# 32 of 256 tokens of an expert layer by gathered rows, the other 224 densely with a fused activation pair

## The chip, the core and the metric

One core of a Trainium2 chip runs the whole program: two transformer blocks on 256 tokens of width 2048, in float32. The metric is the device time of one execution, the median of the runs. The profile is one further execution, taken by the hardware profiler.

## What is computed

The change sits in the last layer of the second block, an expert layer (PEER) with 16384 experts. Each expert is one row of `u_tab` and one row of `v_tab`, 2048 numbers each. Each token picks 16 experts for each of 8 heads, 128 in all:

```python
q = (x @ wq).reshape(B, S, PEER_HEADS, 2, half)
s = jnp.einsum('bshpd,pkd->bshpk', q, subkeys)
s1, i1 = lax.top_k(s[..., 0, :], PEER_TOPK)
s2, i2 = lax.top_k(s[..., 1, :], PEER_TOPK)
...                                   # 16 x 16 candidates, best 16: idx, top_s
gate = jax.nn.softmax(top_s, axis=-1)
ue = jnp.take(u_tab, it, axis=0)      # per token: its 128 rows
ve = jnp.take(v_tab, it, axis=0)
act = gelu(jnp.einsum('td,ted->te', xt, ue))
out = jnp.einsum('te,ted->td', gt * act, ve)
```

The layer's result is added to the residual stream, and a last norm follows.

## The kernel before, in words

Activations lie transposed: 128 features in the partitions, the 256 tokens along the free axis, 16 such tiles for the width of 2048. All large products go through `chunk` and `mm3`. `chunk` (L371 to L385) loads a weight block of 128 x 2048 in two halves on SyncE's queue (`raw`), and for each half makes an upper part `whi` (ScalarE's cast to fp32r, L380) and a rest `wlo` (VectorE's subtraction, L381). Activations are split the same way by `split` (L411 to L420) into an upper and a lower tile (`Ah`, `Al` or `Bh`, `Bl`). `mm3` then runs three fp32r matmuls of 256 columns for each of the 16 steps k: upper x upper (L391), upper weights x lower activations (L392), lower weights x upper activations (L393), all into one PSUM tile. So each step k loads the same upper weights twice and the lower ones once.

`raw`, `whi` and `wlo` have four buffers each (halves), which is two weight blocks. `chunk` is issued with a priority 2000 instructions ahead, so that loads, casts and subtractions run as early as a buffer is free. Otherwise an engine works in the order of the program.

Side work is queued as generators (`push`), and `tick(n)` (L326) issues about n units of it after a large product. A generator that yields `GAP` waits for the next large product.

The expert layer computes all 16384 experts for all tokens and multiplies by a gate matrix that is zero where a token did not pick an expert:
- `route` (L1446): 16 blocks of `w_q`, and for each head the best 16 of both halves on VectorE; `route_tail` (L1492) makes gates and expert numbers from them, as side work behind the first `w_u` blocks.
- `build_g` (L1572): the gate matrix, from one-hot matrices in f16, 16 tokens at a time (`NT`): four VectorE operations and 32 matmuls of 128 columns per tile, 16 tiles. It goes to DRAM as `gdr`. It is side work too, behind further `w_u` blocks.
- `peer_u` (L1604): one block of 128 experts: product, times the norm's factor (L1609, VectorE), gelu (L1611, ScalarE). What is made before the gate matrix is there is stored in DRAM (`stash`, 64 blocks) and loaded again later (`st`, L1656, POOL's queue).
- The main loop in `peer` (L1658 ff.): 8 groups of 16 blocks. Each block is multiplied by its gates `G` (L1651) and split into `A` tiles; groups 0 to 3 take all their blocks from the stash, groups 4 to 7 take theirs from `peer_u`. Then come 16 blocks of `w_v`, whose products are added to the residual `hT` (L1686, VectorE). There is one set of 16 `A` tiles, so that the splits of a group overwrite those of the last one.

Of the kernel before, what the change touches and what calls it, by code (L numbers as in the profile page):

```python
# [48 lines left out]
T8 = 2  # L49
PRE = (60, 64, 64, 64, 80, 96, 112, 128)  # L50
# [12 lines left out]
def _consts():  # L63
# [31 lines left out]
    put("bkt", oh, "A")  # L95
    return {"cst" + g: np.concatenate(c, 1) for g, c in cols.items()}
# [5 lines left out]
def pack(inp):  # L102
# [132 lines left out]
class Kern:  # L235
# [73 lines left out]
    # ---- small helpers  # L309
# [9 lines left out]
    def mmps(self):  # L319
        return self.psm.tile([128, 256], F32, name="mm")  # L320

    # ---- work that is issued between the large products
# [3 lines left out]
    def tick(self, n=1, gaps=True):  # L326
        """spend n on the queued work; what follows a gap waits for the next large product to be issued"""
# [59 lines left out]
    def mm3(self, p, w, x, first=True, last=True):  # L387
        nc = self.nc
        n = len(w)
        for k in range(n):  # L390
            nc.tensor.matmul(p, w[k][0], x[k][0], start=(first and k == 0), stop=False)  # L391
            nc.tensor.matmul(p, w[k][0], x[k][1], start=False, stop=False)  # L392
            nc.tensor.matmul(p, w[k][1], x[k][0], start=False, stop=(last and k == n - 1))  # L393
# [14 lines left out]
    def xtile(self, st, k):  # L408
        return (self.xp.tile([128, 256], F32R, name=f"{st}h{k}"), self.xp.tile([128, 256], F32R, name=f"{st}l{k}"))

    def split(self, st, k, src, gain=None):  # L411
        nc = self.nc
        h, l = self.xtile(st, k)
# [6 lines left out]
        return h, l  # L420
# [19 lines left out]
    def warm_sqrt(self):  # L440
        """the table of the square root is loaded here, ahead of the next rstd"""
# [18 lines left out]
    def log1pexp_neg(self, out, e):  # L460
        """out = log1p(e), 0 <= e <= 1"""
# [15 lines left out]
    def softplus_neg(self, out_log1p, x):  # L477
        """out_log1p = log1p(exp(-|x|))"""
# [6 lines left out]
    def columns(self, r):  # L485
        """the two token columns of a row vector that all partitions hold"""
# [8 lines left out]
    # ---- stage 1  # L495
# [54 lines left out]
    def compress(self, kcs):  # L550
        """hidden layers of the compressed keys in partitions 0..63, of the values in 64..127"""
# [4 lines left out]
        for l in range(16):  # L556
            w = []
            for nm, st in (("k", "h"), ("v", "l")):
                wt = self.xp.tile([128, 256], F32, name=f"B{st}{l}")
                nc.scalar.dma_start(wt, self.I["c1" + nm][l // 8][:, 256 * (l % 8):256 * (l % 8) + 256])  # L560
                w.append(wt)
            wts.append(w)
            if l % 4 == 3:
                yield
# [146 lines left out]
    def nsa_pipe(self):  # L711
        """scores run ahead of the probabilities, these ahead of the output of both heads of a query block"""
# [74 lines left out]
    def nsa_out(self, pair):  # L787
        """both heads of a block, in the two halves of the array's columns"""
# [21 lines left out]
    # ---- RG-LRU  # L810
# [61 lines left out]
    def norm_residual(self, acc, r, gpost, st, gnext, ssq):  # L872
        """h += acc * r * gpost; next operands = split(h * gnext)"""
# [90 lines left out]
    def ple_prep(self):  # L964
# [4 lines left out]
        for k in range(2):  # L969
            h = self.T([128, 256], f"ph{k}", dt=F32R, bufs=1)  # L970
            l = self.T([128, 256], f"pl{k}", dt=F32R, bufs=1)
            nc.scalar.copy(h, pT[:, k])
            nc.vector.tensor_tensor(l, pT[:, k], h, op=ALU.subtract)
            self.px.append((h, l))
# [27 lines left out]
    # ---- block 2 mixers  # L1002
# [6 lines left out]
    def sincos(self, ph, sn, cs, w):  # L1009
        """sin and cos of ph [128, w]; ph is reduced in place"""  # L1010
# [16 lines left out]
    def s5_setup(self):  # L1027
        """tables of the recurrence, its input and its output weights, kept in DRAM until the blocks need them"""
# [153 lines left out]
    def s5_output(self, b, half, X, Y, cw, gw, uT):  # L1182
        """issued amid the next half, when the products are long ready"""
# [124 lines left out]
    def mlstm_cell(self, h, q, k, v, so):  # L1308
# [3 lines left out]
        # state after chunk 0  # L1312
# [122 lines left out]
    # ---- PEER  # L1435
# [10 lines left out]
    def route(self):  # L1446
# [4 lines left out]
        self.gT = [B([128, 256], f"g{i}T", F16) for i in range(2)]  # L1451
        self.rv = [self.T([128, 2, 8, 16], f"rv{i}", bufs=1) for i in range(2)]
        self.ri = [self.T([128, 2, 8, 16], f"ri{i}", dt=U32, bufs=1) for i in range(2)]
        for h in range(8):
# [29 lines left out]
            self.later(rest)  # L1484

# [6 lines left out]
    def route_tail(self):  # L1492
# [52 lines left out]
        for tb in range(2):  # L1545
# [24 lines left out]
            yield  # L1570

    def build_g(self):  # L1572
# [10 lines left out]
        for tb in range(256 // NT):  # L1583
# [20 lines left out]
    def peer_u(self, i):  # L1604
        nc = self.nc
        p = self.mmps()
        self.mm3(p, self.chunk(self.I["w_u"][i]), self.xs)
        t = self.T([128, 256], "pu", pool=self.dp)
        nc.vector.tensor_tensor(t, p, self.rz, op=ALU.mult)  # L1609
        a = self.T([128, 256], "pa", bufs=3, pool=self.dp)  # L1610
        nc.scalar.activation(a, t, AF.Gelu)  # L1611
        return a

    def peer(self):
        nc = self.nc
        self.gdr = self.dr.tile([256 // NT, 128, 128, NT], F32, name="gdr")
        stash = self.dr.tile([PRE[2] // 4, 128, 4, 256], F32, name="stash")
        self.dp = self.pool("dp", 2)
        n = 0
# [114 lines left out]
```

## Time and profile before

| | |
|---|---|
| median of 3 runs | 3413.0 us (3411.52 to 3414.73) |
| span of the profiled execution | 3406.6 us (no other time of it is listed) |
| TensorE busy | 3358.2 us, 99% |
| VectorE busy | 2256.7 us, 66% |
| ScalarE busy | 1678.6 us, 49% |
| GpSimd (POOL) busy | 231.2 us, 7% |
| DMA | 647.75 MB, mean 190 GB/s |

A span runs from the first to the last instruction. PE is TensorE's matmul, PEld its weight load, which runs beside matmuls; DVE is VectorE, ACT ScalarE, POOL GpSimd, SP SyncE. The end of a matmul in the trace is modelled, and its row covers the way through the array, so the spacing of starts says more than the length. A plain f32 matmul is recorded as two. L with a number is a line of the kernel.

### The profile page before, as it was taken

To read this page: it belongs to the slowest core of one execution; us is meant where nothing else is said; L and a number is where in the kernel's file an instruction comes from. 1 tells how busy PE (TensorE), PEld (TensorE's weight loads), DVE (VectorE), ACT (ScalarE), POOL (GpSimd) and SP (SyncE) were. 2 spreads that over 40 slices of the span, in tenths; PEclk is the share of its full clock that TensorE was granted. 3 is DMA by queue.
4 is the path that set the end of the run, shared out by engine and by line. 5 is a ranking of instruction groups with operands and counts; after the bars stand their busy time and mean duration, and the time that the engine had idled before them with its cause. 6 is when DMAs were issued, how large, how long until landed. Compare 5 with 4: busy or idle time off the path is not lost.

```text
span 3406.6 us, 66485 instructions
## 1 busy us (share of the span) xinstructions
PE 3358.2 (99%) x27323; PEld 3267.6 (96%) x27323; DVE 2256.7 (66%) x3763; ACT 1678.6 (49%) x2419; POOL 231.2 (7%) x333
## 2 busy tenths in 40 slices
PE   8999989999999999999999999999999999999998
PEld 7888989999999999888999999999999999999998
DVE  5677786565756488989777976566555655555564
ACT  5567554454645454545554455544434444444343
POOL 2001120000000211000010000000000000000001
PEclk9999999999999999999999999999999999999999
DMA  8443646676766656554465666697676666666664
GB/s 270 126 126 119 181 143 206 203 220 185 229 183 203 184 163 191 159 160 151 138 181 171 209 218 224 229 343 234 189 232 181 185 207 184 208 183 184 182 185 137
DMA packets 197201, 647.75 MB, mean 190 GB/s; under 512 B 22736, under 2 KB 46816, under 8 KB 194848
## 3 DMA queue, kind: packets, MB, share of 16 engines
q1 hardware_dynamic: 171776, 574.69, 55.3%
q0 software_dynamic: 13552, 43.29, 3.7%
q10 hardware_dynamic: 11568, 25.52, 2.0%
q8 instruction: 214, 3.51, 0.4%
q14 instruction: 91, 0.75, 0.1%
HBM read 604.06 MB, written 38.30 MB: 189 GB/s over the span
## 4 chain that ended last, share of the span: by engine, by line
PE 57%; DVE 1%; issue 0%; ACT 0%; DVEq 0%; ACTq 0%
PE mm L391 18%; PE mm L392 18%; PE mm L393 17%; PE sm L1598 2%; PE oT L1192 1%; PE sm L1150 0%; PE sm L1475 0%; DVE hT L1693 0%; PE sm L1203 0%; PE sm L1373 0%; DVE s5Y L1170 0%; PE sm L1338 0%; PE sm L1325 0%; DVE wlo L381 0%; PE sm L1358 0%
## 5 line engine op out<-in xcount | busy, mean ns | idle before, releaser
L380 ACT CAST whi<-raw 128x1024 fp32r<-128x1024 f32 x1056 | 1103.9, 1046 | 1421.3 <-PE mm L392 1254.4
L381 DVE TENSOR_TENSOR wlo<-raw,whi 128x1024 fp32r<-128x1024 f32 x1056 | 1292.4, 1225 | 732.1 <-ACT whi L380 728.8
L391 PE MATMUL mm<-Bh,whi 128*128 128x256 f32 x4240 | 1207.6, 285 | 0.0
L392 PE MATMUL mm<-Bl,whi 128*128 128x256 f32 x4240 | 1201.2, 283 | 0.0
L393 PE MATMUL mm<-Bh,wlo 128*128 128x256 f32 x4240 | 1200.2, 283 | 0.0
L391 PE MATMUL mm<-Ah,whi 128*128 128x256 f32 x4176 | 1187.9, 286 | 12.5 <-ACT Ah L415 5.1
L392 PE MATMUL mm<-Al,whi 128*128 128x256 f32 x4176 | 1187.9, 285 | 2.2 <-DVE Al L419 2.0
L393 PE MATMUL mm<-Ah,wlo 128*128 128x256 f32 x4176 | 1185.2, 284 | 1.2 <-DVE wlo L381 1.2
L391 PEld LDWEIGHTS mm<-Ah,whi 128*128 128x128 f32 x4176 | 803.3, 193 | 23.1 <-issue 6.7
L391 PEld LDWEIGHTS mm<-Bh,whi 128*128 128x128 f32 x4240 | 813.9, 192 | 9.5 <-issue 9.3
L392 PEld LDWEIGHTS mm<-Bl,whi 128*128 128x128 f32 x4240 | 813.8, 192 | 2.3 <-issue 2.2
L393 PEld LDWEIGHTS mm<-Bh,wlo 128*128 128x128 f32 x4240 | 813.4, 192 | 1.1 <-issue 1.0
L392 PEld LDWEIGHTS mm<-Al,whi 128*128 128x128 f32 x4176 | 804.6, 193 | 7.1 <-DVE Al L419 2.8
L393 PEld LDWEIGHTS mm<-Ah,wlo 128*128 128x128 f32 x4176 | 804.6, 193 | 4.6 <-issue 2.0
L431 POOL TENSOR_TENSOR ssq<-ssq,sq 128x256 f32<-128x256 f32 x110 | 125.6, 1141 | 1477.4 <-ACT sq L429 1474.2
L1686 DVE TENSOR_TENSOR hT<-hT,mm 128x256 f32<-128x256 f32 x128 | 53.8, 420 | 88.2 <-PE mm L393 88.2
L1609 DVE TENSOR_TENSOR pu<-mm,rstd 128x256 f32<-128x256 f32 x128 | 54.1, 423 | 56.4 <-PE mm L393 56.4
L415 ACT CAST Ah<-pa 128x256 fp32r<-128x256 f32 x64 | 26.0, 406 | 83.9 <-DVE pa L1651 83.9
L1623 POOL DMA_DIRECT2D stash<-pa x64 | 34.7, 542 | 472.9 <-ACT pa L1611 353.0
L1598 PE MATMUL sm<-gB,gA 128*128 128x128 f16 x512 | 65.8, 297 | 0.0
L1611 ACT ACTIVATE pa<-pu 128x256 f32<-128x256 f32 x128 | 52.9, 413 | 24.3 <-DVE pu L1609 24.1
L1599 ACT ACTIVATE gt<-sm 128x512 f32<-128x512 f32 x64 | 63.2, 1090 | 2.1 <-PE sm L1598 0.9
(432 smaller groups left out, 2165.2 us busy)
## 6 DMA issues: line engine op xcount, KB each, us to landing
raw<-in_w_m SPq DMA_DIRECT2D x256, 512.0 KB, 4.4
raw<-in_w_u SPq DMA_DIRECT2D x256, 512.0 KB, 4.4
raw<-in_w_v SPq DMA_DIRECT2D x256, 512.0 KB, 4.3
raw<-in_w_z SPq DMA_DIRECT2D x156, 512.0 KB, 3.9
raw<-in_w_o SPq DMA_DIRECT2D x64, 512.0 KB, 3.7
raw<-in_w_pg SPq DMA_DIRECT2D x32, 512.0 KB, 4.5
raw<-in_w_q SPq DMA_DIRECT2D x32, 512.0 KB, 4.1
gdr<-gt ACTq DMA_DIRECT2D x16, 1024.0 KB, 4.3
```

What stands on the lines that cost most here:

```text
L380: nc.scalar.copy(hi, raw)
L381: nc.vector.tensor_tensor(lo, raw, hi, op=ALU.subtract)
L391: nc.tensor.matmul(p, w[k][0], x[k][0], start=(first and k == 0), stop=False)
L392: nc.tensor.matmul(p, w[k][0], x[k][1], start=False, stop=False)
L393: nc.tensor.matmul(p, w[k][1], x[k][0], start=False, stop=(last and k == n - 1))
L431: nc.gpsimd.tensor_tensor(st["acc"], st["acc"], st["last"], op=ALU.add)
L1598: nc.tensor.matmul(p[:, 128 * r:128 * r + 128], A[:, q, :, r], b[:, q, :, r], start=(i == 0), stop=(i == 1))
L1599: nc.scalar.activation(Gt[:, :, 4 * q:4 * q + 4].rearrange("p i t -> p t i"), p.rearrange("p (t i) -> p t i", t=4), AF.Copy, scale=1.0 / GSC)
L1609: nc.vector.tensor_tensor(t, p, self.rz, op=ALU.mult)
L1611: nc.scalar.activation(a, t, AF.Gelu)
L1623: nc.gpsimd.dma_start(stash[n // 4, :, n % 4], self.peer_u(n))
L1686: nc.vector.tensor_tensor(self.hT[:, nb], self.hT[:, nb], p, op=ALU.add)
```

## The change

224 tokens (`ND2`) go the dense way, the last 32 (`SP`) by gathered rows.

The dense way: the two parts of an activation now lie in one tile of 2 x 256. In the expert layer `mm2` takes the place of `mm3`: per step k one matmul of the upper weights over both parts (2 x 224 columns, into two areas of one PSUM bank) and one of the lower weights over the upper part (224 columns). The two areas are added afterwards: in `peer_u` by a ScalarE copy and a VectorE add, for `w_v` by two VectorE adds. The activations of the expert layer are normalized in advance and split anew after the last `w_q` block (`xu`). The gate matrix and the stash have 224 tokens; `st` has 3 buffers instead of 4 and is loaded on SyncE's queue.

The gathered way: the expert tables are passed a second time, as rows cut in four quarters of 512. A tile has 32 tokens x 4 quarters in its 128 partitions. For each of a token's 128 experts an indirect DMA on POOL gathers 128 quarter rows (256 KB), and VectorE makes a dot product of them (`u`) or adds them with a weight (`v`). That is 256 gathers, with six buffers, as side work behind the main loop's blocks (`tick(TSP)`). Between both halves come one product over the quarters, gelu and gates; at the end four transposes and four adds into `hT`.

The other stages keep `mm3`, with operands `x[:, 0]` and `x[:, 1]` of the new tile. The core of the diff:

```diff
+SP = 32
+ND2 = 256 - SP
+NQ = 128 // SP
+QW = 2048 // NQ
+NR = 6
+TSP = 1.6
...
+    out["u_rows"] = A(f["peer_u_2"][0]).reshape(16384 * NQ, QW)
+    out["v_rows"] = A(f["peer_v_2"][0]).reshape(16384 * NQ, QW)
...
+    def mm2(self, w, x, n):
+        nc = self.nc
+        p = self.psm.tile([128, 512], F32, name="mm")[:, :2 * n].rearrange("p (c t) -> p c t", c=2)
+        m = len(w)
+        for k in range(m):
+            nc.tensor.matmul(p, w[k][0], x[k][:, :, :n], start=(k == 0), stop=False)
+            nc.tensor.matmul(p[:, 0], w[k][1], x[k][:, 0, :n], start=False, stop=(k == m - 1))
+        return p
...
     def xtile(self, st, k):
-        return (self.xp.tile([128, 256], F32R, name=f"{st}h{k}"), self.xp.tile([128, 256], F32R, name=f"{st}l{k}"))
+        return self.xp.tile([128, 2, 256], F32R, name=f"{st}x{k}")
...
     def route(self):
...
+            for k in range(3 * h - 3, min(3 * h, KC)):
+                if k >= 0:
+                    xn.append(self.xp.tile([128, 2, 256], F32, name=f"Ax{k}")[:, 0])
+                    V.scalar_tensor_tensor(xn[k], self.hT[:, k], self.P("norm2_g_2", k), self.rz, op0=ALU.mult, op1=ALU.mult)
+        self.behind()
+        self.xu = [self.split("B", k, xn[k][:, :ND2]) for k in range(KC)]
+
+        def sparse_x():
+            p = self.ps()
+            for k in range(KC):
+                q, c = divmod(k, KC // NQ)
+                nc.tensor.matmul(p[SP * q:SP * q + SP, 128 * c:128 * c + 128], xn[k][:, ND2:], self.C("ident"), start=True, stop=True)
+            nc.scalar.copy(self.xsp, p[:, :QW])
+
+        self.later(sparse_x)
...
     def route_tail(self):
...
+        yield GAP
+        p = self.ps()
+        for i, src in enumerate((gt[:, 1].rearrange("p s h -> p (s h)"), *es)):
+            nc.tensor.matmul(p[:, 128 * i:128 * i + 128], self.C("rsel"), src, start=True, stop=True)
...
     def build_g(self):
...
-        for tb in range(256 // NT):
+        for tb in range(ND2 // NT):
...
     def peer_u(self, i):
         nc = self.nc
-        p = self.mmps()
-        self.mm3(p, self.chunk(self.I["w_u"][i]), self.xs)
-        t = self.T([128, 256], "pu", pool=self.dp)
-        nc.vector.tensor_tensor(t, p, self.rz, op=ALU.mult)
-        a = self.T([128, 256], "pa", bufs=3, pool=self.dp)
+        p = self.mm2(self.chunk(self.I["w_u"][i]), self.xu, ND2)
+        t = self.T([128, ND2], "pu", pool=self.dp)
+        nc.scalar.copy(t, p[:, 1])
+        nc.vector.tensor_tensor(t, t, p[:, 0], op=ALU.add)
+        a = self.T([128, ND2], "pa", bufs=3, pool=self.dp)
         nc.scalar.activation(a, t, AF.Gelu)
         return a
 
+    def sparse(self, gp):
...
+        def gather(n):
+            r = gp.tile([128, QW], F32, name="row", bufs=NR)
+            nc.gpsimd.indirect_dma_start(out=r, out_offset=None, in_=self.I["uv"[n // 128] + "_rows"],
+                                         in_offset=bass.IndirectOffsetOnAxis(ap=self.osp[:, n % 128:n % 128 + 1], axis=0))
+            rows.append(r)
+
+        n = 0
+        for s in range(256):
+            while n < min(256, s + NR):
+                gather(n)
+                n += 1
+            r = rows.popleft()
+            i = s % 128
+            if s < 128:
+                V.tensor_tensor_reduce(out=r, in0=r, in1=self.xsp, scale=1.0, scalar=0.0, op0=ALU.mult, op1=ALU.add,
+                                       accum_out=d[:, i:i + 1])
+            elif i:
+                V.scalar_tensor_tensor(acc, r, w[:, i:i + 1], acc, op0=ALU.mult, op1=ALU.add)
+            else:
+                V.tensor_scalar(acc, r, w[:, 0:1], None, op0=ALU.mult)
+            yield
+            if s == 127:
+                yield GAP
+                p = self.ps()[:, :128]
+                nc.tensor.matmul(p, self.C("same"), d, start=True, stop=True)
+                nc.scalar.activation(w, p, AF.Gelu)
+                V.tensor_tensor(w, w, self.gsp, op=ALU.mult)
+                yield
...
     def peer(self):
...
+        self.push(self.sparse(gp))
...
         def stashed(i):
-            st = gp.tile([128, 4, 256], F32, name="st", bufs=4)
-            nc.gpsimd.dma_start(st, stash[i])
+            st = gp.tile([128, 4, ND2], F32, name="st", bufs=3)
+            nc.sync.dma_start(st, stash[i])
             return st
...
                         gated(g, n % 16, self.peer_u(n))
                         n += 1
+                    self.tick(TSP)
...
             if g == 7:
+                self.flush()
                 self.warm_sqrt()
             for nb in range(16):
-                p = self.mmps()
-                self.mm3(p, self.chunk(self.I["w_v"][16 * g + nb]), hid)
+                p = self.mm2(self.chunk(self.I["w_v"][16 * g + nb]), hid, ND2)
...
-                nc.vector.tensor_tensor(self.hT[:, nb], self.hT[:, nb], p, op=ALU.add)
+                for c in range(2):
+                    nc.vector.tensor_tensor(self.hT[:, nb, :ND2], self.hT[:, nb, :ND2], p[:, c], op=ALU.add)
...
+                else:
+                    self.tick(TSP)
```

## Rows read from the trace of the kernel before

**Rows 1.** The page: span, and busy time of each engine.
```profile
span 3406.6 us, 66485 instructions
...
PE 3358.2 (99%) x27323; PEld 3267.6 (96%) x27323; DVE 2256.7 (66%) x3763; ACT 1678.6 (49%) x2419; POOL 231.2 (7%) x333
```

**Rows 2.** The page: the chain that ended last, by line.
```profile
PE mm L391 18%; PE mm L392 18%; PE mm L393 17%; PE sm L1598 2%; PE oT L1192 1%; PE sm L1150 0%; PE sm L1475 0%; DVE hT L1693 0%; PE sm L1203 0%; PE sm L1373 0%; DVE s5Y L1170 0%; PE sm L1338 0%; PE sm L1325 0%; DVE wlo L381 0%; PE sm L1358 
```

**Rows 3.** Stretches: us, busy PE PEld DVE ACT POOL (counts), granted clock, DMA share, GB/s.
```profile
1864.00:1910.00 46.00, 46.00 (x386) 46.00 (x385) 45.93 (x197) 24.33 (x29) 3.78 (x7) 1.00 0.59 180
1910.00:1970.00 60.00, 60.00 (x504) 60.00 (x503) 55.74 (x72) 26.55 (x38) 5.96 (x11) 1.00 0.73 222
...
2210.00:3390.00 1180.00, 1180.00 (x9832) 1179.63 (x9831) 672.83 (x868) 496.29 (x630) 35.06 (x44) 1.00 0.66 204
...
2214.00:2299.00 85.00, 85.00 (x710) 85.00 (x710) 56.87 (x93) 38.42 (x55) 7.05 (x13) 1.00 0.98 344
```

**Rows 4.** Timeline of TensorE in the main loop: start us, length us, line.
```profile
2999.93 0.28 PE L391 MATMUL mm<-Ah,whi 128*128 128x256 f32 x1
...
3011.93 0.28 PE L392 MATMUL mm<-Al,whi 128*128 128x256 f32 x1
```

**Rows 5.** Timeline: weight loads of plain f32 matmuls of 512 columns.
```profile
44.22 0.19 PEld L529 LDWEIGHTS sm<-t,cstA 128*128 128x128 f32 x1 [0.24 <-issue]
44.65 0.19 PEld L529 LDWEIGHTS sm<-t,cstA 128*128 128x128 f32 x1 [0.24 <-issue]
```

**Rows 6.** Timeline and lengths (ns, min/median/max) of matmuls of 128 columns.
```profile
1971.77 1.00 PE L1598 MATMUL sm<-gB,gA 128*128 128x128 f16 x7
...
L1598 PE MATMUL sm<-gB,gA x512: 285/297/304, 1970.5 to 2204.1; 128*128 128x128 f16 x171
...
1772.90 0.83 PE L1475 MATMUL sm<-parD,rq 128*128 128x128 f32 x6
...
L1475 PE MATMUL sm<-parD,rq x64: 272/275/348, 1772.6 to 1860.3; 128*128 128x128 f32 x64
```

**Rows 7.** Timeline of VectorE: a turn of groups, an add, a reduce's end.
```profile
2464.22 1.23 DVE L381 TENSOR_TENSOR wlo<-raw,whi 128x1024 fp32r<-128x1024 f32 x1 [0.54 <-ACT whi L380]
2465.36 2.43 DVE L416 TENSOR_TENSOR Al<-st,Ah 128x256 fp32r<-128x256 f32 x7
...
2474.47 0.75 DVE L1651 TENSOR_TENSOR st<-st,G 128x256 f32<-128x256 f32 x2
...
1869.91 0.60 DVE L1500 TENSOR_TENSOR rcd<-rv,rv 128x448 f32<-128x448 f32 x1
...
130.06 0.08 DVE L752 DVE_READ_ACCUMULATOR2_ANT mn<- 128x1 f32 x1
```

**Rows 8.** Groups at 2210 to 3390 us: count, busy us, mean ns, idle before.
```profile
L381 DVE TENSOR_TENSOR wlo<-raw,whi 128x1024 fp32r<-128x1024 f32 x407 | 498.4, 1225 | 342.0 <-ACT whi L380 342.0
L380 ACT CAST whi<-raw 128x1024 fp32r<-128x1024 f32 x407 | 426.1, 1047 | 578.4 <-PE mm L392 537.2 <-issue 21.6 <-DMA raw<-in_w_v 14.4
...
L1656 POOL DMA_DIRECT2D st<-stash x16 | 8.5, 535 | 205.4 <-DVE Al L416 193.3 <-DMA gdr<-gt 7.7 <-issue 4.5
```

**Rows 9.** Waits: TensorE's of the span, POOL's in the main loop.
```profile
PE mm L391 <- ACT Ah L418: 4.6, 1, 4.6
...
POOL st L1656 <- DVE Al L416: 193.3, 10, 88.1
```

**Rows 10.** DMA at 2400 to 2600 us, then 2214 to 2300: us to landing.
```profile
DMA packets 12720, 40.69 MB, mean 203 GB/s; under 512 B 1296, under 2 KB 3344, under 8 KB 12702
...
raw<-in_w_v SPq DMA_DIRECT2D x69, 512.0 KB, 4.2
...
DMA packets 14354, 29.32 MB, mean 341 GB/s; under 512 B 1266, under 2 KB 9202, under 8 KB 14345
...
raw<-in_w_v SPq DMA_DIRECT2D x20, 512.0 KB, 6.7
...
st<-stash POOLq DMA_DIRECT2D x4, 512.0 KB, 6.6
```

More of the change, by code (lines that the diff above doesn't have):

```diff
@@ L95, in _consts @@
     put("bkt", oh, "A")
+    t, q = p % SP, p // SP
+    put("rsel", (np.arange(128)[:, None] == 128 - SP + t[None, :]).astype(np.float32), "P")
+    put("same", (t[:, None] == t[None, :]).astype(np.float32), "P")
+    put("qcol", q.astype(np.float32)[:, None], "P")
     return {"cst" + g: np.concatenate(c, 1) for g, c in cols.items()}
@@ L319, in mmps @@
     def mmps(self):
-        return self.psm.tile([128, 256], F32, name="mm")
+        return self.psm.tile([128, 512], F32, name="mm")[:, :256]
     def push(self, gen, q=0):
@@ L390, in mm3 @@
         for k in range(n):
-            nc.tensor.matmul(p, w[k][0], x[k][0], start=(first and k == 0), stop=False)
-            nc.tensor.matmul(p, w[k][0], x[k][1], start=False, stop=False)
-            nc.tensor.matmul(p, w[k][1], x[k][0], start=False, stop=(last and k == n - 1))
+            nc.tensor.matmul(p, w[k][0], x[k][:, 0], start=(first and k == 0), stop=False)
+            nc.tensor.matmul(p, w[k][0], x[k][:, 1], start=False, stop=False)
+            nc.tensor.matmul(p, w[k][1], x[k][:, 0], start=False, stop=(last and k == n - 1))
+    def mm2(self, w, x, n):
[6 more added lines that the diff above has]
+        return p
     def blocks(self, srcs, x, first=2):
@@ L556, in compress @@
         for l in range(16):
[L557 to L562, printed above, removed]
+            wt = self.xp.tile([128, 2, 256], F32, name=f"Bx{l}")
+            for s, nm in enumerate("kv"):
+                nc.scalar.dma_start(wt[:, s], self.I["c1" + nm][l // 8][:, 256 * (l % 8):256 * (l % 8) + 256])
+            wts.append(wt)
             if l % 4 == 3:
@@ L576, in compress @@
             for s in range(2):
-                nc.tensor.matmul(p[64 * s:64 * s + 64], blk[:, l, s], wts[l][s], start=(l == 0), stop=(l == 15))
+                nc.tensor.matmul(p[64 * s:64 * s + 64], blk[:, l, s], wts[l][:, s], start=(l == 0), stop=(l == 15))
         hid = self.T([128, 256], "chid", bufs=1)
@@ L969, in ple_prep @@
         for k in range(2):
[L970 to L974, printed above, removed]
+            x = self.T([128, 2, 256], f"px{k}", dt=F32R, bufs=1)
+            nc.scalar.copy(x[:, 0], pT[:, k])
+            nc.vector.tensor_tensor(x[:, 1], pT[:, k], x[:, 0], op=ALU.subtract)
+            self.px.append(x)
     def ple_proj(self, half):
@@ L1611, in peer_u @@
         nc.scalar.activation(a, t, AF.Gelu)
         return a
+    def sparse(self, gp):
+        nc = self.nc
+        V = nc.vector
+        d = self.T([128, 128], "spd", bufs=1, pool=gp)
+        w = self.T([128, 128], "spw", bufs=1, pool=gp)
+        acc = self.T([128, QW], "spa", bufs=1, pool=gp)
+        rows = deque()
+        def gather(n):
[24 more added lines that the diff above has]
+                V.tensor_tensor(w, w, self.gsp, op=ALU.mult)
+                yield
+        yield GAP
+        p = self.ps()
+        nb = QW // 128
+        for i in range(nb):
+            nc.tensor.transpose(p[:, 128 * i:128 * i + 128], acc[:, 128 * i:128 * i + 128], self.C("ident"))
+        for i in range(nb):
+            h = self.hT[:, i:KC:nb, ND2:]
+            V.tensor_tensor(h, h, p[:, 128 * i:128 * i + 128].rearrange("p (q t) -> p q t", q=NQ), op=ALU.add)
+        yield
@@ L1614, in peer @@
     def peer(self):
         nc = self.nc
[L1616 to L1617 removed]
+        NB = ND2 // NT
+        self.gdr = self.dr.tile([NB, 128, 128, NT], F32, name="gdr")
+        stash = self.dr.tile([PRE[2] // 4, 128, 4, ND2], F32, name="stash")
         self.dp = self.pool("dp", 2)
+        self.ctab = dict(self.ctab)
+        self.load_tabs(self.dp, "P")
+        self.gsp = self.T([128, 128], "gsp", bufs=1, pool=self.dp)
@@ L1639, in peer @@
         gp = self.pool("gp", 2)
-        GP = 256 // NT // 8
+        self.push(self.sparse(gp))
         def load_g(g, i, eng):
             if i == 0:
-                Gs[g] = gp.tile([128, 256 // NT, 16, NT], F32, name="G")
-            b = slice(GP * i, GP * i + GP)
-            eng.dma_start(Gs[g][:, b], self.gdr[b, :, 16 * g:16 * g + 16].rearrange("b p i t -> p b i t"))
+                Gs[g] = gp.tile([128, NB, 16, NT], F32, name="G")
+            b = slice(2 * i, min(2 * i + 2, NB))
+            if b.start < NB:
+                eng.dma_start(Gs[g][:, b], self.gdr[b, :, 16 * g:16 * g + 16].rearrange("b p i t -> p b i t"))
         def gated(g, j, a):
```

13 lines of the change are left out of this document (11 added, 2 removed).

## The prediction, made before the changed kernel ran

> **What bounds the kernel now.** I read the page first, then the chain, then a table of stretches, then single matmuls. The page has TensorE busy for 99% of a span of 3406.6 us [rows 1]; since a busy matmul row also covers waiting inside the array, that alone is no proof. The chain of waits gives the three matmul lines of `mm3` 53% of the span, and everything else in it is small [rows 2]. By stretches, TensorE is busy without a gap in the expert layer (its main loop is 2210 to 3390 us), at a granted clock of 1.00, the upper level of 2.4 GHz, while VectorE is busy 57% of its main loop and the DMA engines 66% [rows 3]. The timeline shows why: one matmul starts every 0.12 us without exception (2999.93 to 3011.93 us: 100 starts, 120.0 ns) [rows 4]. A weight block has 48 of them, 5.76 us. 256 blocks (1474.6 us) and the 512 one-hot products of `build_g` (at 117 ns, 60 us) make 1535 us; that is the layer. So time is worth what it saves TensorE here, as long as nothing else becomes late.
>
> What sets the 120 ns? Plain f32 matmuls of 512 columns start every 430 ns, two passes of 0.42 ns a column, and the load of the next 128 weight columns is hidden [rows 5]. A single-pass matmul of 256 columns would so need 108 ns. Matmuls of 128 f16 columns (54 ns of streaming) still start 117 ns apart ((1.00 - 0.297)/6), and plain ones of 128 columns (107 ns) 111 ns apart ((0.83 - 0.275)/5) [rows 6]. So each 128-column weight load holds its matmul to 111 to 120 ns, and shorter ones gain nothing below that.
>
> **The products.** Per step k, 3 loads with 768 columns become 2 loads with 448 and 224. The wide one: 448 x 0.42 = 188 ns, above the load, which it hides (200 if the 12 ns by which 120 exceeds 108 are a fixed charge per matmul). The narrow one: 94 ns of streaming, below the load of the next weights: 120 ns, the row of its own kind (112 to 120). So 308 ns instead of 360 (bounds 300 to 320), and 52 x 16 x 256 blocks = **-213 us** (-246 to -164). A block takes 4.93 us.
>
> By the Trainium skill, page "TensorE: Matmul & The Clock Gate", section "Back-to-back issue gap", a warm gap is N/2.4 + 2.5 ns: 109 ns before, 285 ns per step after. The trace has 120 where it says 109, so the load it leaves out does count. Its result is the third rival.
>
> **The dense rest.** `build_g` makes 14 tiles, not 16: 64 products less, -7.5 us. New on TensorE: 16 f32 products for `sparse_x`, 3 for the routing, 4 transposes and one more, about 48 passes at 0.112 = +5.4. TensorE's floor: 3406.6 - 213 - 7.5 + 5.4 = 3191.5 us.
>
> **What must stay hidden.** VectorE's recorded durations overlap: a `wlo` of 1.23 us lets the next start after 1.14, seven splits of 256 columns take 2.43 us (0.335 each), an add of 448 columns is 0.60 long, 0.52 by that overlap, and a reduce reads its accumulator in 0.08 more [rows 7]. So: split, gate or add of 224 columns 0.30 to 0.33; a gathered row's dot product 0.69 (0.61 + 0.08); its weighted add 0.61 to 0.67. `tick(1.6)` puts 1.6 of these, 1.1 us, behind each block, about 162 blocks for the 258 steps. VectorE per ticked block: `w_v` 2.28 + 2 x 0.33 + 1.1 = 4.04 us; `w_u` 2.28 + 3 x 0.30 + 1.1 = 4.28; `w_v` of the groups that also gate stashed blocks 4.64. Against 4.93 that is 82 to 94%: hidden on average, but the cover is thin, where before a `w_v` block left half of VectorE free.
>
> Five things come through:
> - The operands `xu` overwrite those of the last `w_q` block, so the first `w_u` block waits for its splits. The same kind of hand-over cost 4.6 us once [rows 9]: **+4.6** (0 to 15).
> - Route tail: VectorE is full at 1864 to 1910 (45.9 of 46) and nearly so to 1970 [rows 3]. Its 18.5 blocks could save 15 us; VectorE lets through 4. **+11** (0 to 15).
> - Four groups of stashed blocks: 16 splits follow each other at the turn of a group; they took 9.1 us (2465.36 to 2474.47) [rows 7] and the next group's last step came just in time. With 9.9 us for two blocks, less the lead, and sparse steps between: 2 us each, **+8** (0 to 25). In this the moved loads count: `st` goes from POOL, where it waited 193 us in all [rows 9] with nothing behind it, to SP with one buffer fewer; behind it queue the `raw` loads, which ACT's cast, `wlo` and L393's successor wait for. Only the fourth load of a group can wait, for the first quad's splits.
> - The weight ring. Four `raw` halves serve two blocks: landing, cast (1.05), `wlo` (1.2) must fit in 9.86 us instead of 11.5. Traffic rises: 256 gathers of 262 KB, 1.6 per block, are 85 GB/s on top of 213 for weights and some 14 for G (14.7 MB over the loop): 310. Landing was 4.2 us at 203 GB/s and 6.7 at 341 [rows 10], so about 6.2 here: 6.2 + 1.05 + 1.2 [rows 8] = 8.5, which leaves 1.4 for queueing behind a 0.7 us sparse step. At 344 GB/s TensorE had no gap [rows 3], but with 11.5 us. I take 0.15 us per ticked block, **+24** (0 to 110).
> - Sparse steps wait for gathers, and `wlo` queues behind them. No indirect load is in the trace. Below: a POOL issue, 0.54 us [rows 8]; above: issue and landing one after the other, 0.54 + 6.6 = 7.1 [rows 8, 10]. Six rows are in flight, so I take 1.2 us each against a need of one per 3.2 us: hidden, **+2** for the first ones.
>
> The page "DMA: Bandwidth & Descriptors" of the Trainium skill, section on the SWDGE path, has 2.0 us + bytes/436e3 per such DMA, an estimate of 2.6 us here; no run yet shows one, and by it too the gathers would keep up.
>
> Elsewhere `x[:, 0]` and the wider PSUM tile change addresses only; ACT, busy 496 of 1180 us [rows 3], gets one short copy per `w_u` block and stays below 60% of the shorter loop.
>
> Sum: 3191.5 + 4.6 + 11 + 8 + 24 + 2 = 3241 us of span. The median of the runs, 3413.0, is 6.4 above the profiled span (no time of that execution itself is listed): **3248 us**.
>
> **Rivals.**
> 1. *The narrow matmul loses its single pass* (slower). All single-pass rows have 256 columns; none is narrower, so no row excludes it. For: nothing but that gap. Against: f16 and plain f32 keep their cost per column at 128. Done as plain f32 it would be two records of 188 ns, +256 ns on 4096 steps: 4297 us; one record of 188: 3526. It decides from 160 ns per narrow matmul (165 us / 4096 = 40 above 120).
> 2. *The ring or VectorE binds.* Landing of 7 us and 2 us of queueing make 11.2 per two blocks, 5.6 per block: 162 x (0.67 - 0.15) = +84: 3332 us. For: the cover computed above. Against: no gap at 344 GB/s.
> 3. *Loads don't bind.* 672 x 0.42 = 282 ns per step: 106 us less, 3141 us. Against: the floor of [rows 6]. The gap rule of the Trainium skill quoted above ("TensorE: Matmul & The Clock Gate") would come out beside it, at 285 ns.
> 4. *The gathers don't keep up* (slower in the end). If issue and landing follow each other, 256 x 7.1 = 1818 us instead of 823: 4243 us. It decides from 3.86 us per gather ((823 + 165)/256). Against: six buffers.
>
> **Numbers.** Forecast 0.62, ring 0.18, loads free 0.06, narrow pass 0.07, gathers 0.07 (half of it beyond 3.86 us). Forecast's own range 3190 to 3300; with rivals 2 and 3: 3140 to 3350. Under 0.2% (7 us) can't be told from no change. Faster 0.62 + 0.18 + 0.06 + 0.02 = 0.88, same 0.02, slower 0.10.
>
> **What would show it.** Wide matmuls 188 ns ahead of the next start, narrow ones 112 to 120; TensorE's gaps in the main loop under 5%, at group turns and behind `wlo`; VectorE near 85% there; gathers at one per 3.2 us, landing under 10 us; `raw` landing near 6.2. A narrow matmul over 160 ns, or sparse steps waiting on DMA for most of the loop, would make the forecast wrong.

## The result, and the profile after

The changed kernel took 3510.4 us (3508.9 to 3513.9), the kernel before 3412.3 us on the same chip: a ratio of 1.029, interval 1.028 to 1.031. It is slower by 98 us; forecast were 165 less.

First the page of the changed kernel: span, busy times, three of the rows by fortieths, and the two groups of matmuls with the most idle time before them.

```profile
span 3508.3 us, 59745 instructions
...
PE 3261.7 (93%) x23207; PEld 3084.0 (88%) x23207; DVE 2456.9 (70%) x4306; ACT 1700.8 (48%) x2558; POOL 514.2 (15%) x573
...
PE   8999989999999999999998999558999757999998
...
POOL 2001210000000120000100001672000573000002
PEclk9999999999999999999999999769999878999999
...
L415 PE MATMUL mm<-Bx,wlo 128*128 128x224 f32 x2048 | 574.3, 280 | 147.7 <-DVE wlo L393 116.0
...
L415 PE MATMUL mm<-Ax,wlo 128*128 128x224 f32 x2048 | 548.3, 268 | 28.2 <-DVE wlo L393 18.0
```

TensorE's work fell by 97 us, but it is busy only 93% of the span, against 99% [rows 1]. The loss is not spread: the row PE has two holes, and in the same two places POOL is busy and the granted clock drops. The narrow matmul, which alone needs the low half `wlo`, had 176 us of idle time before it (147.7 + 28.2), most of them waiting for `wlo`. Away from the holes, a timeline of TensorE (start us, length us) answers [rows 4]:

```profile
3099.90 0.38 PE L414 MATMUL mm<-Ax,whi 128*128 128x448 f32 x1
3100.11 0.26 PE L415 MATMUL mm<-Ax,wlo 128*128 128x224 f32 x1
3100.22 0.37 PE L414 MATMUL mm<-Ax,whi 128*128 128x448 f32 x1
3100.43 0.26 PE L415 MATMUL mm<-Ax,wlo 128*128 128x224 f32 x1
3100.53 0.38 PE L414 MATMUL mm<-Ax,whi 128*128 128x448 f32 x1
```

Two steps take 0.63 us here (3099.90 to 3100.53), with 0.21 from the start of a wide matmul to the next and 0.10 to 0.11 from a narrow one. Over the 639 steps at 3000 to 3200 us the mean is 313 ns, against 360. The dense part does what the change says. Now three stretches of equal length (the columns are those of [rows 3]); the first two are the holes:

```profile
2200.00:2390.00 190.00, 106.25 (x401) 91.38 (x402) 126.23 (x325) 38.02 (x66) 139.33 (x134) 0.70 0.87 284
2750.00:2940.00 190.00, 110.14 (x490) 97.66 (x490) 136.57 (x199) 44.22 (x74) 146.91 (x122) 0.76 0.82 257
3000.00:3190.00 190.00, 190.00 (x1215) 181.21 (x1214) 127.05 (x171) 96.69 (x133) 0.00 (x0) 1.00 0.69 219
```

190 us hold 1215 matmuls where nothing is late; the holes have 401 and 490. At the full rate these would have taken 63 and 77 us, so 127 + 113 = 240 us are lost there. TensorE stands idle for 164 of them (84 + 80); the other 76 are longer matmuls, at a granted clock of 0.70 and 0.76. VectorE is busy for only 66% and 72% of the holes, and yet it is what TensorE waits for. Its timeline shows how that goes together (in brackets the idle time before an instruction, and what ended it):

```profile
2329.26 1.22 DVE L393 TENSOR_TENSOR wlo<-raw,whi 128x1024 fp32r<-128x1024 f32 x1
2330.40 0.68 DVE L1685 CUSTOM_DVE_ANT_0 row<-row,xsp 128x512 f32<-128x512 f32 x1
...
2331.44 0.69 DVE L1685 CUSTOM_DVE_ANT_0 row<-row,xsp 128x512 f32<-128x512 f32 x1 [0.35 <-DMA row<-in_u_rows,osp]
...
2332.82 0.69 DVE L1685 CUSTOM_DVE_ANT_0 row<-row,xsp 128x512 f32<-128x512 f32 x1 [0.68 <-DMA row<-in_u_rows,osp]
...
2336.14 0.69 DVE L1685 CUSTOM_DVE_ANT_0 row<-row,xsp 128x512 f32<-128x512 f32 x1 [2.63 <-DMA row<-in_u_rows,osp]
...
2336.81 0.69 DVE L1685 CUSTOM_DVE_ANT_0 row<-row,xsp 128x512 f32<-128x512 f32 x1
...
2337.48 0.69 DVE L1685 CUSTOM_DVE_ANT_0 row<-row,xsp 128x512 f32<-128x512 f32 x1
...
2338.10 1.22 DVE L393 TENSOR_TENSOR wlo<-raw,whi 128x1024 fp32r<-128x1024 f32 x1
```

Six dot products stand between two low halves, three of them wait for their gathers, and the second `wlo` runs 8.84 us after the first, where TensorE needs one every 2.5 us. The second `wlo` could have run long before: ScalarE had made the upper parts of both halves by 2325.29 us.

```profile
2323.32 1.97 ACT L392 CAST whi<-raw 128x1024 fp32r<-128x1024 f32 x2
```

The written program puts 1.6 sparse steps behind each block of two low halves. But VectorE's queue isn't in the written order, against what the section on the kernel before says of the engines: the language's scheduler lays it out, and here the sparse steps stand ahead of their places. All 128 dots run at 2190 to 2390 us and the weighted adds at 2750 to 2940 us, with mostly 3 to 6 of them between two low halves. Groups and waits of the first hole, and one gather at its shortest:

```profile
L1685 DVE CUSTOM_DVE_ANT_0 row<-row,xsp 128x512 f32<-128x512 f32 x121 | 80.9, 692 | 66.0 <-DMA row<-in_u_rows,osp 56.8 <-issue 8.3 <-DVE spd L1685 0.7
...
L1673 POOL DMA_INDIRECT row<-in_u_rows,osp x117 | 127.7, 1091 | 37.7 <-issue 29.9 <-DVE spd L1685 6.5 <-DVE st L1751 0.6
...
PE mm L415 <- DVE wlo L393: 47.1, 15, 7.7
...
2241.93 0.95 POOL L1673 DMA_INDIRECT row<-in_u_rows,osp  x1 [0.30 <-issue]
```

121 dots have 81 us of work and 66 us of waiting; POOL spends 1.09 us on a gather and 0.32 idle before it, 1.25 in all at best. With the stores of stashed blocks in the same queue one gather comes every 1.56 us (190/122: these 117 and the first 5 of `v`), and VectorE could use one every 0.67. POOL is at its own pace here: of the 38 us idle before gathers, 30 have no cause that the profile shows, and only 6.5 are waits for a dot that frees a row.

By the Trainium skill, page "PSUM — Partial Sum Buffer", section "Engine vs sequencer instructions", VectorE's queue is strictly first in, first out. The trace agrees: for 2.63 us VectorE stood before a dot whose gather had not landed, while the `wlo` behind it had its data since 2325.29.

### The profile page after: what moved, and what is told of

It is laid out like the page before. It is cut to its first block, busy times and chain, and to the rows that moved or that the text cites. A ratio compares the mean times of both kernels' runs of the same rounds, so it can differ in the third digit from the quotient of the medians.

```text
span 3508.3 us, 59745 instructions
## 1 busy us (share of the span) xinstructions
PE 3261.7 (93%) x23207; PEld 3084.0 (88%) x23207; DVE 2456.9 (70%) x4306; ACT 1700.8 (48%) x2558; POOL 514.2 (15%) x573
## 4 chain that ended last, share of the span: by engine, by line
PE 43%; DVE 5%; DMA 4%; issue 4%; POOL 3%; ACT 0%; DVEq 0%; POOLq 0%; SPq 0%; ACTq 0%
PE mm L414 21%; PE mm L415 10%; PE mm L403 3%; PE mm L404 3%; PE mm L405 3%; POOL row L1673 3%; DMA row<-in_v_rows,osp 2%; DVE wlo L393 1%; PE sm L1646 1%; PE oT L1214 1%; DMA row<-in_u_rows,osp 1%; DVE spa L1688 1%; DMA st<-stash 0%; DVE Ax L441 0%; DVE row L1685 0%
## 5 line engine op out<-in xcount | busy, mean ns | idle before, releaser
L415 PE MATMUL mm<-Bx,wlo 128*128 128x224 f32 x2048 | 574.3, 280 | 147.7 <-DVE wlo L393 116.0
L414 PE MATMUL mm<-Bx,whi 128*128 128x448 f32 x2048 | 707.3, 400 | 1.6 <-ACT whi L392 0.9
L414 PE MATMUL mm<-Ax,whi 128*128 128x448 f32 x2048 | 661.3, 382 | 16.5 <-DVE spa L1688 10.8
L403 PE MATMUL mm<-Bx,whi 128*128 128x256 f32 x2192 | 625.1, 285 | 0.0
L404 PE MATMUL mm<-Bx,whi 128*128 128x256 f32 x2192 | 621.6, 284 | 0.0
L405 PE MATMUL mm<-Bx,wlo 128*128 128x256 f32 x2192 | 620.9, 283 | 0.0
L403 PE MATMUL mm<-Ax,whi 128*128 128x256 f32 x2128 | 608.4, 288 | 13.2 <-ACT Ax L440 5.1
L404 PE MATMUL mm<-Ax,whi 128*128 128x256 f32 x2128 | 608.3, 286 | 3.1 <-DVE Ax L444 3.0
L405 PE MATMUL mm<-Ax,wlo 128*128 128x256 f32 x2128 | 605.7, 285 | 1.2 <-DVE wlo L393 1.2
L415 PE MATMUL mm<-Ax,wlo 128*128 128x224 f32 x2048 | 548.3, 268 | 28.2 <-DVE wlo L393 18.0
L415 PEld LDWEIGHTS mm<-Bx,wlo 128*128 128x128 f32 x2048 | 422.0, 206 | 163.8 <-DVE wlo L393 128.6
L414 PEld LDWEIGHTS mm<-Bx,whi 128*128 128x128 f32 x2048 | 416.3, 203 | 37.6 <-ACT whi L392 1.2
L414 PEld LDWEIGHTS mm<-Ax,whi 128*128 128x128 f32 x2048 | 393.4, 192 | 49.3 <-DVE spa L1688 11.2
L403 PEld LDWEIGHTS mm<-Ax,whi 128*128 128x128 f32 x2128 | 410.0, 193 | 24.0 <-issue 6.9
L403 PEld LDWEIGHTS mm<-Bx,whi 128*128 128x128 f32 x2192 | 420.3, 192 | 9.5 <-issue 9.3
L415 PEld LDWEIGHTS mm<-Ax,wlo 128*128 128x128 f32 x2048 | 400.1, 195 | 30.5 <-DVE wlo L393 19.3
L404 PEld LDWEIGHTS mm<-Bx,whi 128*128 128x128 f32 x2192 | 420.6, 192 | 2.3 <-issue 2.2
L405 PEld LDWEIGHTS mm<-Bx,wlo 128*128 128x128 f32 x2192 | 420.4, 192 | 1.1 <-issue 1.0
L404 PEld LDWEIGHTS mm<-Ax,whi 128*128 128x128 f32 x2128 | 411.6, 194 | 7.5 <-DVE Ax L444 4.0
L405 PEld LDWEIGHTS mm<-Ax,wlo 128*128 128x128 f32 x2128 | 411.4, 193 | 4.5 <-issue 2.0
```

Source lines behind the costliest of these rows:

```text
L403: nc.tensor.matmul(p, w[k][0], x[k][:, 0], start=(first and k == 0), stop=False)
L404: nc.tensor.matmul(p, w[k][0], x[k][:, 1], start=False, stop=False)
L405: nc.tensor.matmul(p, w[k][1], x[k][:, 0], start=False, stop=(last and k == n - 1))
L414: nc.tensor.matmul(p, w[k][0], x[k][:, :, :n], start=(k == 0), stop=False)
L415: nc.tensor.matmul(p[:, 0], w[k][1], x[k][:, 0, :n], start=False, stop=(k == m - 1))
```

## The experiments

Theory A: the loss is the order, 4 to 6 sparse steps between two low halves, each waiting for a gather. Rivals: B, the gathers cost wherever they stand; C, the dense part costs; D, VectorE's total of sparse time costs. All ratios below are against runs of the kernel before on the same chip (3408.8 to 3412.6 us); a difference between two versions is one of medians, some of them from different chips.

**No sparse work** (e_dense).

```diff
-        self.push(self.sparse(gp))
```

Expected: 

> The sparse work of the 32 tokens is left out altogether (no gathers, no dots, no weighted adds; the expert layer's contribution of these tokens is missing). Theory A (the dense part works as forecast, and the loss is that the sparse steps stand in two bursts in VectorE's queue, 4 to 6 between two low halves of the weights, each waiting on a gather): before's 3412 - 184 (4096 steps at 315 instead of 360 ns) - 7.5 (build_g) + some 15 (hand-over of the new operands): 3235, between 3220 and 3260. Rival C (the dense part itself costs: its two additions per block, the copy, the 512-column results): over 3380. If the clock alone were the cause, it would be low here too.

Measured: 3274.2 us (ratio 0.960, 0.959 to 0.962). C falls: the dense part alone is 135 us faster than before. It is 14 us over the range, for stretches that a later section names.

**Sparse steps tied in their places** (e_pin). The added call makes an instruction follow, in its engine's queue, the one written before it; it adds no wait.

```diff
-                V.tensor_tensor_reduce(...)       # likewise for the two other forms
+                op = V.tensor_tensor_reduce(...)
+            self.tc.keep_in_program_order(op)
```

Expected: 

> Everything is computed; each sparse step on VectorE is tied behind the instruction written before it on that engine, so that it can't be moved ahead, and 1.6 of them stand behind each block. Theory A: the bursts are gone, one gather per 3 us, TensorE stays fed: 3240 to 3290. Rival B (the gathers' pace on POOL or their share of the transfers costs, wherever they stand): 3400 to 3520. Rival D (VectorE's total of sparse time, 258 x 0.65 us, is what is lost, in whatever order): 3400 or more.

Measured: 3309.7 us (0.971, 0.969 to 0.972), 200 us under the changed kernel with the same work. B and D fall. The same stretches as above, of this kernel:

```profile
2200.00:2390.00 190.00, 177.81 (x1075) 166.96 (x1076) 158.06 (x304) 88.50 (x130) 78.65 (x71) 0.95 0.93 321
2750.00:2940.00 190.00, 185.66 (x1169) 175.86 (x1168) 158.72 (x222) 89.98 (x121) 78.20 (x59) 0.99 0.87 294
```

1075 and 1169 matmuls instead of 401 and 490, although VectorE is busy for longer (83 and 84%). Its timeline has one or two adds, then both low halves of a block together:

```profile
2680.92 0.75 DVE L1688 SCALAR_TENSOR_TENSOR spa<-row,spw,spa 128x512 f32<-128x512 f32 x1
2681.58 2.35 DVE L393 TENSOR_TENSOR wlo<-raw,whi 128x1024 fp32r<-128x1024 f32 x2
...
2685.84 1.53 DVE L1688 SCALAR_TENSOR_TENSOR spa<-row,spw,spa 128x512 f32<-128x512 f32 x2
2687.30 2.35 DVE L393 TENSOR_TENSOR wlo<-raw,whi 128x1024 fp32r<-128x1024 f32 x2
```

**No gathers, in the order of the bursts** (e_nogather), and **no gathers, tied** (e_pin_nogather).

```diff
-            nc.gpsimd.indirect_dma_start(out=r, ...)
-   ...tensor_tensor_reduce(out=r, in0=r, in1=self.xsp, ...)        # and r in both adds
+   ...tensor_tensor_reduce(out=r, in0=self.xsp, in1=self.xsp, ...)
```

Expected of the first: 

> The 256 gathers are left out and the 256 sparse steps multiply one row that is there already (the contribution of the 32 tokens is wrong); their order in VectorE's queue is still that of two bursts. Theory A with waits on gathers as the larger part: the first burst is 11 dots of 0.61 us to a block beside some 3.8 us of other work, 10.5 us a block for 12 blocks, so +65; the second 4 adds of 0.75 us, 6.8 us a block for 32 blocks, so +55 at most: 3300 to 3360, so 150 to 210 of the loss are waits on gathers. Rival D (VectorE's own time in the bursts is the whole loss): 3450 to 3510. Rival B (gathers alone, order does not matter): 3230 to 3260.

Expected of the second: 

> Both edits: no gathers, and the sparse steps tied in their places, 1.6 behind each block (the contribution of the 32 tokens is wrong). Theory A: 3235 to 3260, within 30 of the version with gathers in the same order. Rival B: 150 to 250 under the version with gathers. Rival D: 3400 or more.

Measured: 3381.8 us (0.992, 0.990 to 0.993) and 3300.0 us (0.968, 0.967 to 0.970). So the order costs 82 us even where nothing is gathered. The first is 22 us over the expected range, the second 40: waits on gathers are a smaller part of the loss than expected, 129 us instead of 150 to 210 (3510 - 3382), and in the tied order gathers add 10 us. The bursts of the first of these two kernels are shorter (dots at 2184 to 2310 us, adds at 2666 to 2805). A stretch of 50 us in each:

```profile
2200.00:2250.00 50.00, 36.40 (x170) 30.88 (x171) 50.00 (x138) 17.82 (x34) 3.23 (x6) 0.85 0.70 231
...
2700.00:2750.00 50.00, 35.90 (x168) 30.31 (x167) 49.04 (x73) 14.55 (x25) 0.00 (x0) 0.84 0.35 116
```

Without waits VectorE is full, 50.00 and 49.04 of 50 us: it is then its own work in the burst that makes `wlo` late, for a shorter time.

**A quarter of the bytes per gather** (e_quarter).

```diff
-    out["u_rows"] = A(f["peer_u_2"][0]).reshape(16384 * NQ, QW)     # v_rows likewise
+    out["u_rows"] = A(f["peer_u_2"][0]).reshape(16384 * 16, 128)
-            r = gp.tile([128, QW], F32, name="row", bufs=NR)
+            r = gp.tile([128, 128], F32, name="row", bufs=NR)
...                                     # dot and add read the 128 numbers four times
```

Expected: 

> As the changed kernel with its two bursts, but each gather fetches rows of 128 numbers instead of 512, from the wrong place (the dot and the add read the 128 four times, as 512 columns, so VectorE's time stays; the contribution of the 32 tokens is wrong). It splits the 128 us that gathers cost in the bursts (3510 against 3382 without them). Theory A1 (POOL's pace, 1.36 to 1.6 us per gather, is what the dots wait for): POOL takes as long for a quarter of the bytes, and the time stays within 40 of 3510. Theory B1 (the transfers: 33.7 MB in 190 us crowd the weights and land late): 3380 to 3430.

Measured: 3493.6 us (1.024, 1.022 to 1.025). Its first hole, and POOL's group in it:

```profile
2200.00:2390.00 190.00, 116.63 (x448) 100.41 (x448) 130.96 (x327) 41.67 (x71) 143.82 (x132) 0.70 0.51 164
...
L1675 POOL DMA_INDIRECT row<-in_u_rows,osp x119 | 136.8, 1149 | 36.6 <-issue 21.0 <-DVE spd L1688 9.5 <-DMA row<-in_u_rows,osp 3.0
```

The DMA share falls from 0.87 to 0.51, POOL takes 1.15 us per gather where it took 1.09, and the time falls by 17 us only. So of the 129 us that gathers cost in the bursts, about 112 don't go with the bytes; with POOL at its own pace in the hole, they are put down to that pace.

The Trainium skill, page "Perfetto Trace Analysis", section "DMA Instruction — SWDGE (GPSIMD)", says that POOL's interval for such a DMA ends when its descriptors are made, not when the data has moved. This trace agrees: the interval does not shrink with the bytes (1.15 us, against 1.09).

**All 256 tokens in two matmuls** (e_256), and **224 tokens in three** (e_pin_three).

```diff
-ND2 = 256 - SP
+ND2 = 256                    # and no sparse work
```

```diff
-            nc.tensor.matmul(p, w[k][0], x[k][:, :, :n], ...)
-            nc.tensor.matmul(p[:, 0], w[k][1], x[k][:, 0, :n], ...)
+            nc.tensor.matmul(p, w[k][0], x[k][:, 0, :n], ...)       # on the tied version;
+            nc.tensor.matmul(p, w[k][0], x[k][:, 1, :n], ...)       # one add, no copy
+            nc.tensor.matmul(p, w[k][1], x[k][:, 0, :n], ...)
```

Expected of the first: 

> All 256 tokens take the dense path with the wide and the narrow matmul (512 and 256 columns), no sparse work: everything is computed. It tells what one pass over the high half saves by itself. Theory P (the forecast's: a matmul has a fixed part, and two for three saves one of them): 335 to 345 ns per step instead of 360, so 3412 - 4096 x 0.015 to 0.025 + some 45 (hand-over and group turns as in the version without sparse work): 3340 to 3390. Theory Q (the 315 ns are 672 columns at 0.469 ns, as the 360 ns are 768 at 0.469: nothing is saved by fusing): 358 to 362 ns, 3440 to 3470, slower than before.

Expected of the second: 

> As the version with tied sparse steps, but the products of the 224 tokens are three matmuls of 224 columns into one result, with one addition per block and the activation read straight from the result (no copy, no second addition). Everything is computed. Theory P: three fixed parts instead of two, 3 x 107 = 320 ns or more, 20 us and more over the tied version (3310): 3325 to 3350. Theory Q: 315 ns as before it, and VectorE is lighter by 0.4 us a block, so that low halves come sooner at the group turns: 3280 to 3310, not slower than the tied version.

Measured: 3378.2 us (0.991, 0.989 to 0.992) and 3410.5 us (1.000, 0.999 to 1.001). The timelines of TensorE, first of the kernel with 256 tokens:

```profile
3000.07 0.39 PE L414 MATMUL mm<-Bx,whi 128*128 128x512 f32 x1
3000.30 0.28 PE L415 MATMUL mm<-Bx,wlo 128*128 128x256 f32 x1
3000.42 0.39 PE L414 MATMUL mm<-Bx,whi 128*128 128x512 f32 x1
```

then of the one with three matmuls:

```profile
2700.13 0.27 PE L414 MATMUL mm<-Ax,whi 128*128 128x224 f32 x1
2700.24 0.28 PE L415 MATMUL mm<-Ax,whi 128*128 128x224 f32 x1
2700.36 0.27 PE L416 MATMUL mm<-Ax,wlo 128*128 128x224 f32 x1
2700.47 0.27 PE L414 MATMUL mm<-Ax,whi 128*128 128x224 f32 x1
```

Over stretches without a gap a step takes 350 ns with 512 and 256 columns (571 steps at 3000 to 3200 us) and 335 with three times 224 (448 steps at 3150 to 3300). Q falls in both. P's direction holds; 3378 us is in its range, but the step of 350 ns and the second time are outside: fusing alone saves 10 ns of 360, fewer columns alone 25, and both together 47. So 22 ns a step are the fusing at 224 columns, 4096 x 22 = 90 us, and the second version's 3410 is the tied version's 3310 plus these, to within 10.

**Fewer steps per block** (e_pin_late): the tied version with one number changed.

```diff
-TSP = 1.6
+TSP = 1.35
```

Expected: 

> The tied version with 1.35 sparse steps per block instead of 1.6, so that they are spread over 190 blocks instead of 160; everything is computed. Theory A with what is left at the group turns (transfers at 0.9 and more of the time where the stashed blocks come back): the turns are relieved a little, 3295 to 3310. If the sparse steps' share of VectorE were what costs the last 36 us over the version without them, it would not change: 3310.

Measured: 3305.4 us (0.969, 0.967 to 0.971); the interval overlaps that of the tied version. The medians are 4 us apart.

**Every step of the layer tied** (e_tie_all), with 1.35 steps per block.

```diff
-                c = next(q[0])
+                last = next(i for i in reversed(self.nc.cur_bb.bb.instructions) if i.engine == self.dve)
+                with self.tc.issue_after(last):         # in the expert layer
+                    c = next(q[0])
```

Expected: 

> As the tied version with 1.35 steps per block (3305), and everything else that is issued in steps behind the blocks of the expert layer (route's heads and tail, build_g) is tied in the same way on VectorE. Everything is computed. Theory A carried on: at 1860 to 2000 us the small steps of the routing stand ahead of low halves in VectorE's queue just as the sparse ones did, and TensorE is short by some 18 us there, with the clock at 0.93 to 0.97; tied, most of it comes back: 3280 to 3298. If the loss there is the hand-over of the 16 new operands or VectorE's total in that stretch, nothing changes: 3300 to 3315, or longer, since the routing then ends later.

Measured: 3297.6 us (0.967, 0.965 to 0.969): the fastest complete version, though its interval overlaps that of e_pin_late. The reason isn't shown. Here is the stretch at issue, first of e_pin_late:

```profile
1850.00:2000.00 150.00, 134.36 (x833) 0.93 0.55 178
```

then of this version (us, TensorE busy, clock, DMA share, GB/s):

```profile
1850.00:2000.00 150.00, 133.12 (x847) 0.98 0.57 186
```

TensorE is idle there as long as before; only the clock is better.

**A later start of the sparse steps** (e_pin_start; e_tie_start has this and the edit before).

```diff
-        self.push(self.sparse(gp))
+            if g == 0:                       # behind the first group's blocks
+                self.push(self.sparse(gp))
-TSP = 1.6
+TSP = 1.45
```

Expected of the first: 

> As the tied version, but the first sparse step stands behind the first group's blocks instead of ahead of them, with 1.45 steps per block; everything is computed. Theory: at 2150 to 2250 us the first group's table, its stashed blocks and the first gathers come together (transfers 0.97 of the time, 332 GB/s, TensorE busy 43 of 50 us at a clock of 0.86); without the gathers there it is as in the version without sparse work (44 of 50, 0.90) and some 5 to 10 us come back: 3295 to 3308. If the gathers cost through VectorE's share, nothing: 3305 to 3315.

Expected of the second: 

> Both edits together, everything computed: if both reasons hold, 3270 to 3295; if neither does, 3305 to 3315.

Measured: 3312.3 us (0.971, 0.970 to 0.973) and 3314.1 us (0.971, 0.969 to 0.973). Nothing comes back. But this does not clear the first gathers: the edit moved the dots (the first at 2270 us instead of 2211), while the first six gathers are still issued at 2184 to 2191 us. What the turn is like without them stands in the trace of the tied version without gathers. First this version, then that one (TensorE busy, clock, DMA share, GB/s):

```profile
2150.00:2250.00 100.00, 85.47 (x523) 0.91 0.84 289
...
2150.00:2250.00 100.00, 89.60 (x549) 0.95 0.83 280
```

In front of the first stashed block VectorE waits 13.2 us in the first and 9.3 in the second, so some 4 us of the turn are likely these six gathers. With every step tied, the later start is 16 us slower than without it (3314 against 3298, with 1.45 steps per block instead of 1.35); the reason isn't shown, and it leaves the gain of e_tie_all in doubt.

**The stash loads on POOL again** (e_tie_pool), on the version with every step tied.

```diff
-            nc.sync.dma_start(st, stash[i])
+            nc.gpsimd.dma_start(st, stash[i])
```

Expected: 

> As the version with all steps tied (3298), but the 32 loads of stashed blocks are issued by POOL again, as before the change, behind the gathers in its queue. Everything is computed. Theory of the forecast's term for the group turns (the stash loads, moved into SP's queue, stand ahead of weight loads and delay them): weights come sooner at the turns, 5 to 15 us back: 3283 to 3293. Rival (the transfers themselves fill the 16 DMA engines there, 0.9 to 0.98 of the time, whichever queue issues them): 3293 to 3303. Rival (a stash load waits in POOL's queue behind gathers that wait for VectorE to free a row): slower, 3305 to 3330.

Measured: 3315.0 us (0.972, 0.970 to 0.974), 17 us slower, in the last rival's range. There are 16 such loads in the trace, not 32. VectorE's waits for them at 2350 to 2600 us, first here, then in e_tie_all (us, times, longest):

```profile
DVE st L1759 <- DMA st<-stash: 19.0, 5, 6.8
...
DVE st L1759 <- DMA st<-stash: 8.4, 4, 2.4
```

So the loads in POOL's queue do come later there. At the first turn it is otherwise: VectorE waits 8.7 us for them instead of 17.7, but 15.3 for a load of gates, and TensorE is busy for 78 of the 100 us at 2150 to 2250 instead of 85. The last rival so has part of the loss; the rest isn't explained. In this form of the kernel SP's queue is the better one.

## Why the prediction was wrong

The step that failed is the assumption in the part on what must stay hidden: "`tick(1.6)` puts 1.6 of these, 1.1 us, behind each block, about 162 blocks for the 258 steps". It was read from the program. In VectorE's queue there were mostly 3 to 6 steps between two low halves instead. From there the cover of 82 to 94% is wrong for the holes and right for the tied version (83 and 84%). No row quoted ahead of the prediction shows the order, but the trace of before has it on a small scale, around an add that [rows 7] quotes. In the program all searches of `route_head` (L1443) stand ahead of the steps of `route_tail` (L1499, L1500); VectorE ran one of them behind two such steps:

```profile
1869.51 0.28 DVE L1499 TENSOR_TENSOR rcd<-rv,rv 128x128 f32<-128x128 f32 x1
...
1870.51 0.28 DVE L1443 FIND_INDEX8 ri<-rv,rs 128x8 uint32<-128x128 f32 x1
```

The time, from kernel to kernel: 3274 dense, +26 for sparse steps in their places, +10 for gathers there (3310), and +200 for the bursts (3510). The 200 are 82 of order with VectorE full, and 3510 - 3382 - 10 = 118 more for the gathers in that order, most of it POOL's pace.

Step by step:
- **The products, 308 ns.** 313 ns, inside the 300 to 320, so -192 us instead of -213; +21 on the forecast. The parts were off in opposite senses: 0.21 us behind the wide matmul instead of 188 ns, 0.10 behind the narrow one instead of 120 ns. So 111 ns is no floor for a matmul behind a wide one; that the sum came out near is in part luck.
- **Narrow matmul's single pass** (rival 1): kept, 0.10 us.
- **Hand-over and route tail, +15.6.** At 1850 to 2000 us the version without sparse work has TensorE idle for 18 us, at a clock of 0.96:

```profile
1850.00:2000.00 150.00, 131.80 (x832) 0.96 0.55 177
2150.00:2250.00 100.00, 90.33 (x556) 0.95 0.84 288
```

- **Group turns, +8.** The second row: 10 us at the first group's turn alone. That "only the fourth load of a group can wait" is wrong: in the dense version VectorE waits 8.92 us for the first, and the next `wlo` stands behind it:

```profile
2197.91 0.99 DVE L1750 TENSOR_TENSOR st<-st,G 128x224 f32<-128x224 f32 x3 [8.92 <-DMA st<-stash]
```

- **The dense kernel as a whole.** With the clock and some 7 us of idle time at 2350 to 2550, it is 32 us over what the forecast's terms without sparse work give (3191.5 + 23.6 + 6.4 + 21 for the products = 3242). The version with 256 tokens, at 350 ns a step, has almost none of it (at 1850 to 2000 us TensorE is busy for 148.9 of 150, at 2150 to 2250 for all 100); that longer blocks are the reason is likely and was not tried by itself.
- **Ring and gathers, +24 and +2.** Sparse work in its places costs 36 (3310 - 3274), 10 of them for gathers.
- **Gathers at 1.2 us.** 1.25 us at best, 1.56 in the hole; all but those 10 us hidden where one is needed every 3.2 us, nearly as forecast.

3248 + 21 + 32 + 10 = 3311 leads to the tied version (3310), as it must, since the 32 and the 10 are taken from measured times: the terms of the sum were 62 us short, and the order was the other 200. Rivals 2 and 4 each named half of what happened, a bound on VectorE and gathers that don't keep up. Both took the even spread for given, so that rival 4 put its point of decision at 3.86 us per gather, where in the bursts 1.56 was too slow.

What stays open: why the version with every step tied is faster than e_pin_late, if it is, why a later start undoes that, and how the 36 us divide among the turns.

## What to carry to other kernels

Work that is written evenly between blocks need not be queued evenly: look at how many low-priority instructions stand between two that feed the critical engine, and tie them there. Whether a queue follows the program can be read from the trace of the kernel before, by two instructions of side work and their places in the program. An engine that is 70% busy can hold up another when what it waits for stands ahead of what the other waits for. A gathered transfer is sized by the pace at which its engine issues it, and that pace matters only against the densest stretch in which it is asked for.

## What the runs showed of the hardware

TensorE's cost per matmul fell less than its columns: 120 ns at 256 [rows 4], 112 at 224 (335/3), 7% for 12.5%. The same 224 columns behind a matmul of 448 cost 0.10 us.

The clock made the holes deeper. After a wait of 3.78 us for `wlo` in the first hole, with a granted clock of 0.70 over the stretch, the timeline is:

```profile
2339.73 0.60 PE L414 MATMUL mm<-Bx,whi 128*128 128x448 f32 x1
...
2340.32 0.60 PE L414 MATMUL mm<-Bx,whi 128*128 128x448 f32 x1
```

A step takes 0.59 us (2339.73 to 2340.32) instead of 0.31: the lower of the two levels, 1.2 GHz. The 76 us in the holes that are lost but not idle fit this.
